# Moving the check for overfull experts into the last expert, and padding narrow tiles to 128 bytes

## The chip, the cores and the metric

The kernel runs on one NeuronCore of a Trainium2 chip. The metric is the device time of one execution in microseconds (us). TensorE (PE) does the matrix products, VectorE (DVE) and ScalarE (ACT) the elementwise work, SyncE (SP) issues nearly all transfers, and GpSimd (POOL) does a few small things.

## The reference, cut to what matters

Two decoder blocks of two layers each run on 256 tokens of width 1024. The last layer's feed-forward is a mixture of eight experts, and it is there that the change moves work:

```python
def moe_swiglu(xn, router, wg, wu, wd):
    t = xn.reshape(B * S, D)
    logits = (t @ router).astype(jnp.float32)
    top_val, top_idx = lax.top_k(logits, TOP_K)          # TOP_K = 2
    gates = jax.nn.softmax(top_val, axis=-1)
    combine = jnp.sum(jax.nn.one_hot(top_idx, N_EXPERTS) * gates[..., None], axis=1)
    out = jnp.zeros_like(t)
    for e in range(N_EXPERTS):                            # 8 experts, inner width 3584
        out = out + combine[:, e:e + 1] * swiglu(t, wg[e], wu[e], wd[e])
    return out.reshape(B, S, D)
```

All of it is float32. A gated residual with its own 1024 x 1024 matrix and a last norm follow.

## The kernel before

**Weights.** Every weight matrix is laid out beforehand in tiles of 512 x 512 (1 MB) in the order in which they are used (class Plan). `ahead` keeps up to five tiles in flight from HBM into `raw` buffers and splits each, half a tile at a time, into a high part (`hi`, a cast on ACT, L435) and a rest (`lo`, a subtraction on DVE, L436). There are five hi and five lo buffers. `mm3` then does three matmuls per block of 128 rows (L450, L451, L452): high by high, rest of the activations by high, high by rest of the weights. Activations are the stationary operand, split in the same way, weights the moving one, 512 columns wide. One tile is twelve matmuls.

**Buffers.** SBUF is cut by pools, one after the other in the order in which they open. A slot takes its bytes per partition, rounded up to 32. `n` tiles (split activations with a gain) come from a pool near the start. `l` tiles (other split activations and much else) come from the pool `lg`, which opens anew in each stage behind the pools `sec` and `sc`, and `x` tiles (the last expert's products) from `lx`. `sec`, from the second block on, holds a tile `half` of 8 bytes; `sc` of the experts' stage holds six narrow tiles that together take 288 bytes. So `l` tiles start at a multiple of 128 bytes in the first block, 32 bytes past one in the second block up to the experts, and 64 past one in the experts, as do `x` tiles.

**Experts.** At most 128 tokens are gathered for each expert (`gather`), so one pass of 128 rows does it if no expert has more. For each of seven chunks of 512 inner columns, `experts` multiplies by the gate matrix (`mg`) and the up matrix (`mu`), two tiles each, into PSUM tiles `a` from a pool of four. ACT's Silu (L1557) and a DVE product (L1559) join them, four transposes on PE (L484) with a split (L492 on ACT, L493 on DVE) turn the product over, and one chunk later `both` multiplies by two tiles of the down matrix (`md`) into two PSUM tiles y. These come from the pool of four `m` tiles, which also serves transposes and gathers. After the last chunk `scatter` splits y (L1503 on ACT, L1504 on DVE), spreads it over the tokens with eight matmuls (L1508, L1509) and adds it to x (L1511).

The seventh expert (e == MID, which is 6) ends in another way: its last chunk's down products follow at once, all outstanding tasks are drained (L1627), and `overflow` loads the largest token count into a register of every engine (L1628) and branches on it (L1661). Where some expert has over 128 tokens, a long body of some 330 instructions per expert on PE and on SP does the rest; with these inputs it is skipped. The way past it has waits of its own: each engine waits for its own earlier work to be complete, and SP for its transfers. The last expert then does its up products, all its down products after them (`finish`), and the final gate.

From the third chunk of the seventh expert on, `raw` has four buffers instead of twelve.

**What sets the order.** PE's order is as the program is written. On the other engines a scheduler moves instructions, but not past a branch. `push` queues generators, `step` and `slot` advance them between products, `need` advances them until a condition holds, `drain` until none is left.

Of the kernel before, what the change touches and what calls it, by code (L numbers as in the profile page):

```python
# [8 lines left out]
F32 = mybir.dt.float32  # L9
# [70 lines left out]
class Plan:  # L80
# [76 lines left out]
    def moe(self):  # L157
        def up(e, c):
            for key, w in (("mg", "moe_w_gate_2"), ("mu", "moe_w_up_2")):
                for g in range(2):  # L160
                    self.add((key, e, c, g), "w3", (w, 0, e), g * 512, g * 512 + 512, c * 512, 512)

        def down(e, c, h):
            self.add(("md", e, c, h), "w3", ("moe_w_down_2", 0, e), c * 512, c * 512 + 512, h * 512, 512)

        def gate(c, g):
            self.add(("pg", c, g), "w3", ("ple_gate_2", 1), g * 512, g * 512 + 512, c * 512, 512)

        prev = None
        for e in range(N_EXP):  # L170
            for c in range(N_FF):
                up(e, c)
                if prev:
                    for h in range(2):
                        down(*prev, h)
                prev = (e, c) if e < N_EXP - 1 else None
                if c == N_FF - 1 and e == MID:
                    for h in range(2):
                        down(e, c, h)
                    prev = None  # L180
        for h in range(2):
            for c in range(N_FF):
                if h and c == LATE:
                    gate(0, 0)
                down(N_EXP - 1, c, h)
        if LATE == N_FF:
            gate(0, 0)
        gate(1, 0)
        gate(0, 1)
        gate(1, 1)  # L190
# [109 lines left out]
class Kernel:  # L300
    def __init__(self, tc, io, ctx):
        self.tc = tc
        self.nc = tc.nc
        self.io = io
        pool = lambda name, bufs, **k: ctx.enter_context(tc.tile_pool(name=name, bufs=bufs, **k))
        self.const = pool("const", 1)
        self.raw_p = pool("raw", RAW)
        self.hi_p = pool("hi", NSPLIT)
        self.lo_p = pool("lo", NSPLIT)
        self.sm = pool("sm", 40)  # L310
        self.na = pool("na", 8)
        self.acc_p = pool("acc", 4, space=PSUM)
        self.ms_p = pool("ms", 4, space=PSUM)
        self.scope = None
        self.plan = Plan()
        self.specs = self.plan.specs
        self.n_dma = self.n_split = self.n_used = 0
        self.rawt = {}
        self.split = {}
        self.flip = 0  # L320
        self.urgent = []
        self.tasks = []
        self.now = 0
        self.rate = 2
        self.grain = GRAIN1
        self.fetching = 0
        self.ring = deque([self.raw_p] * RAW)
        self.queue = None
# [70 lines left out]
    def M(self, *shape):  # L399
        return self.ms_p.tile([128, *(shape or (512,))], F32, tag="m", name="m")  # L400

    def A(self):
        return self.acc_p.tile([128, 512], F32, tag="a", name="a")

    def xs(self, b, h):
        return self.xt[b][h]
# [206 lines left out]
    def fetch(self, name, dt=F32, pool=None):  # L613
        nc, src = self.nc, self.io["c_" + name]
        queue = self.queue or nc.gpsimd
        n = src.shape[1]
        t = (pool or self.sc).tile([128, n], dt, name=name)
        self.fetching += 1

        def gen():  # L620
            yield 3
            if dt == F32:
                queue.dma_start(t, src)
            else:
                for c in range(0, n, 384):
                    m = min(384, n - c)
                    r = self.T((128, m))
                    queue.dma_start(r, src[:, c:c + m])
                    nc.gpsimd.tensor_copy(t[:, c:c + m], r)
                    yield 1  # L630
            self.fetching -= 1
        self.push(gen())
        return t
# [755 lines left out]
    def route(self, norm, ms):  # L1389
        nc = self.nc  # L1390
        small = lambda name, shape, dt=F32: self.sc.tile([128, *shape], dt, name=name)
        self.comb, self.rank, self.sel = small("comb", (2, 8)), small("rank", (2, 8)), small("sel", (2, 8))
        self.count, self.most = small("count", (8,), I32), small("most", (1,), I32)
        self.rst = small("rst", (3, 2), BF16)
        self.unit = small("unit", (128,), BF16)
        nc.vector.tensor_copy(self.unit, self.ident)
        self.rows = [[[small(f"x{n}{b}{h}", (512,), BF16) for n in range(3)] for h in range(2)] for b in range(2)]
        self.need(lambda: ms[2] == 4)
        for h in range(2):
            for b in range(2):  # L1400
                self.thirds(self.xs(b, h), self.rows[b][h], self.T())
        self.spin(SPIN)
        with self.soon(HPR):
            top, s0, s1 = self.pick(ms[:2])

        def rest():
            yield 2
            cnt = self.M(8)
            for b in range(2):
                nc.tensor.matmul(cnt, self.ones, self.sel[:, b], start=b == 0, stop=b == 1)  # L1410
            self.thirds(norm.rst, [self.rst[:, n] for n in range(3)], self.S(2))
            e, g = self.S(2, 2), self.S(2, 2)
            R = norm.ready()
            for b in range(2):
                nc.vector.tensor_scalar(e[:, b, 0:1], top[:, b, 1:2], top[:, b, 0:1], R[b], op0=ALU.subtract, op1=ALU.mult)
            nc.scalar.activation(e[:, :, 1], e[:, :, 0], AF.Exp)
            nc.vector.tensor_scalar(e[:, :, 0], e[:, :, 1], 1.0, None, op0=ALU.add)
            nc.vector.reciprocal(g[:, :, 0], e[:, :, 0])
            nc.vector.tensor_mul(g[:, :, 1], g[:, :, 0], e[:, :, 1])
            for b in range(2):  # L1420
                nc.vector.tensor_scalar(s0[:, b], s0[:, b], g[:, b, 0:1], None, op0=ALU.mult)
                nc.vector.scalar_tensor_tensor(self.comb[:, b], s1[:, b], g[:, b, 1:2], s0[:, b], op0=ALU.mult, op1=ALU.add)
            most = self.S(1)
            nc.vector.tensor_reduce(most, cnt, axis=AX.X, op=ALU.max)
            nc.vector.tensor_copy(self.count, cnt)
            nc.vector.tensor_copy(self.most, most)
        self.push(rest())
# [96 lines left out]

    def both(self, y, e, c, fT, res):
        if c == 0:
            y.extend([self.M(), self.M()])
        for h in range(2):
            self.down(y[h], e, c, h, fT)
            if c == N_FF - 1:  # L1530
                self.push(self.scatter(e, y[h], h, res))

    def experts(self, inner):
# [4 lines left out]
        for e in range(N_EXP):  # L1538
# [2 lines left out]
            y, ft = [], []  # L1541
            for c in range(N_FF):
                for nm in ("mg", "mu"):
                    a = self.A()
                    for g in range(2):
                        w = self.take((nm, e, c, g))
                        self.need(lambda: act[g] is not None)
                        hi, lo = act[g]
                        for j in range(4):
                            self.mm3(a, hi[:, j], lo[:, j], *w[j], g == 0 and j == 0, g == 1 and j == 3)  # L1550
                        if g == 0:
                            self.slot()
# [17 lines left out]
                pend = (y, e, c, fT, here) if e < N_EXP - 1 else None  # L1570
                if c == 2 and e == N_EXP - 2:
                    self.ring = deque([self.raw_p] * RAW)
                if c == 4 and e < N_EXP - 1:
                    res, gen = self.gather(e + 1, 0)
                    self.push(gen)
            if e == MID:
                self.both(*pend)
                pend = None
                inner.close()
                self.overflow()  # L1580
                self.inner(self.scope, lx=2 * N_FF - 2)
        return ft, here

    def finish(self, ft, here, pp, nxt, last):
# [4 lines left out]

        def gate(c, g, b, w):  # L1590
            if (c, b) not in acc:
                acc[c, b] = self.A()
            self.need(lambda: nxt.act[b][g] is not None)
            ah, al = nxt.act[b][g]
            for j in range(4):
# [1 line left out]
            self.slot()  # L1597

        for h in range(2):
            y = self.M()  # L1600
            for c in range(N_FF):
                if h and c == LATE:
                    w = self.take(("pg", 0, 0))
# [20 lines left out]

    def overflow(self):
        nc, io = self.nc, self.io
        self.drain()  # L1627
        n = nc.values_load(self.most[0:1, 0:1], min_val=0, max_val=256)  # L1628

        def wt(key, j):  # L1630
# [4 lines left out]
        def one(e):  # L1635
# [5 lines left out]
            for c in range(N_FF):  # L1641
                accs = []
                for w in ("mg", "mu"):
                    a = self.A()
                    for k in range(8):
                        nc.tensor.matmul(a, act[k // 4][0][:, k % 4], wt((w, e, c, k // 4), k % 4),
                                         start=k == 0, stop=k == 7)
# [10 lines left out]
                for _ in self.scatter(e, y[h], h, res):  # L1658
                    pass

        with self.tc.If(n > 128):  # L1661
            for e in range(N_EXP):
                ne = nc.values_load(self.count[0:1, e:e + 1], min_val=0, max_val=256)
                with self.tc.If(ne > 128):
                    with self.tc.tile_pool(name="ov", bufs=4) as pool, self.tc.tile_pool(name="scp", bufs=4) as self.scp:
                        keep = self.lg, self.oh
                        self.lg = self.oh = pool
                        one(e)
                        self.lg, self.oh = keep


def program(tc, io, stages=("all",)):
# [73 lines left out]


MANUAL = {mybir.EngineType.PE}


def constants():
# [74 lines left out]
```

## Time and profile before

| what | value |
|---|---|
| time, median of 3 runs | 2497.12 us (2496.11 to 2497.93) |
| the profiled execution's own time | 2501.25 us |
| its span, first to last instruction | 2499.4 us |
| PE busy in it | 2464.4 us, 99% |
| DVE busy | 1922.3 us, 77% |
| ACT busy | 1618.6 us, 65% |
| weights and other bytes moved | 600.16 MB, mean 240 GB/s |

The table is the page's first part. A busy PE is not a PE at its peak: matmuls overlap, and a matmul's length is a model. Two matmuls of 512 columns start some 0.23 us apart while each is shown as 0.39 or 0.40 us long. A loss is therefore read from starts, from the idle time in square brackets, and from the granted clock.

### The profile page before, as it was taken

Reading aid. Unit: us, or ns where it says so; the run is one execution under the profiler, and the core shown is the slowest. Engines: PE = TensorE matmul, PEld = TensorE weight load, DVE = VectorE, ACT = ScalarE, POOL = GpSimd, SP = SyncE. Lnnn points to the kernel's source line nnn. Section 1 sums busy time; section 2 is a strip of 40 time slices with the busy share of each in tenths; the row PEclk is TensorE's granted clock in tenths of the full one; section 3 lists DMA queues with packets and bytes.
Section 4 is the critical chain, followed back from the end, with each engine's and each line's share of the span. In section 5 each row is a group of like instructions: output and inputs, shape, how many; then the busy total and the mean of one; then the engine's idle time right before and its main releaser. Section 6 shows DMA issues by size and latency. Waiting matters only on the chain. (4 is left out here: it accounts for less than half of the span.)

```text
span 2499.4 us, 33937 instructions
## 1 busy us (share of the span) xinstructions
PE 2464.4 (99%) x12113; PEld 2040.2 (82%) x12113; DVE 1922.3 (77%) x3330; ACT 1618.6 (65%) x2667; POOL 47.5 (2%) x66
## 2 busy tenths in 40 slices
PE   9999999999999999999999999999999999999998
PEld 7888888888888887888888878888888888888786
DVE  7775765578667656775576879999898989898888
ACT  7555555575556546654557567777777777777675
POOL 1000000100000002000001000000000000000000
PEclk9999999999999999999999989999999999999999
DMA  7443555553345555344564469999899999977895
GB/s 277 158 146 125 179 178 188 198 201 144 135 152 191 175 176 200 106 169 169 199 214 162 166 273 354 356 354 361 342 348 357 353 356 349 361 285 290 322 342 194
DMA packets 90530, 600.16 MB, mean 240 GB/s; under 512 B 12576, under 2 KB 14368, under 8 KB 19568
## 3 DMA queue, kind: packets, MB, share of 16 engines
q1 hardware_dynamic: 84240, 591.27, 64.2%
q10 hardware_dynamic: 4928, 3.16, 0.5%
q0 software_dynamic: 1184, 3.48, 0.4%
q8 instruction: 97, 1.59, 0.2%
q14 instruction: 81, 0.66, 0.1%
HBM read 596.82 MB, written 1.05 MB: 239 GB/s over the span
## 5 line engine op out<-in xcount | busy, mean ns | idle before, releaser
L436 DVE TENSOR_TENSOR lo<-raw,hi 128x512 fp32r<-128x512 f32 (+3 forms) x1584 | 1384.2, 911 | 315.9 <-ACT hi L435 296.7
L435 ACT CAST hi<-raw 128x512 fp32r<-128x512 f32 (+3 forms) x1584 | 1198.2, 800 | 422.6 <-PE a L451 340.1
L450 PE MATMUL a<-hi,n 128*128 128x512 f32 (+2 forms) x2176 | 867.9, 399 | 4.6 <-PEq L1661 3.5
L452 PE MATMUL a<-lo,n 128*128 128x512 f32 (+2 forms) x2176 | 848.9, 390 | 0.0
L451 PE MATMUL a<-hi,n 128*128 128x512 f32 (+2 forms) x2176 | 845.7, 389 | 1.7 <-DVE n L503 1.7
L452 PEld LDWEIGHTS a<-lo,n 128*128 128x128 f32 x2176 | 410.4, 189 | 93.3 <-DVE lo L436 5.1
L451 PEld LDWEIGHTS a<-hi,n 128*128 128x128 f32 x2176 | 411.7, 189 | 81.5 <-DVE n L503 3.2
L450 PEld LDWEIGHTS a<-hi,n 128*128 128x128 f32 x2176 | 411.1, 189 | 81.8 <-issue 4.2
L450 PE MATMUL a<-hi,l 128*128 128x512 f32 x552 | 220.3, 399 | 0.0
L452 PE MATMUL a<-lo,l 128*128 128x512 f32 x552 | 216.2, 392 | 0.0
L451 PE MATMUL a<-hi,l 128*128 128x512 f32 x552 | 216.1, 391 | 0.0
L492 ACT CAST l<-m 128x512 fp32r<-128x512 f32 (+1 forms) x126 | 70.2, 559 | 150.8 <-PE m L484 150.8
L450 PE MATMUL m<-hi,l 128*128 128x512 f32 x400 | 158.9, 397 | 0.7 <-ACT l L492 0.7
L451 PE MATMUL m<-hi,l 128*128 128x512 f32 x400 | 158.3, 396 | 0.2 <-DVE l L493 0.2
L452 PE MATMUL m<-lo,l 128*128 128x512 f32 x400 | 158.1, 395 | 0.0
L493 DVE TENSOR_TENSOR l<-m,l 128x512 fp32r<-128x512 f32 (+1 forms) x126 | 82.5, 658 | 62.4 <-ACT l L492 62.3
L452 PEld LDWEIGHTS a<-lo,l 128*128 128x128 f32 x552 | 103.7, 188 | 23.2
L451 PEld LDWEIGHTS a<-hi,l 128*128 128x128 f32 x552 | 103.8, 188 | 21.1
L450 PEld LDWEIGHTS a<-hi,l 128*128 128x128 f32 x552 | 103.7, 188 | 21.0
L484 PE MATMUL m<-ident,t 128*128 128x128 f32 x652 | 99.0, 272 | 2.8 <-DVE t L567 2.1
L484 PEld LDWEIGHTS m<-ident,t 128*128 128x128 f32 x652 | 80.3, 140 | 22.4 <-DVE t L567 2.6
L450 PEld LDWEIGHTS m<-hi,l 128*128 128x128 f32 x400 | 75.2, 188 | 18.4 <-ACT l L492 0.9
(302 smaller groups left out, 1784.7 us busy)
## 6 DMA issues: line engine op xcount, KB each, us to landing
raw<-in_w_dram SPq DMA_DIRECT2D x553, 1024.0 KB, 5.1
raw<-in_w_dram SPq DMA_DIRECT2D x10, 512.0 KB, 3.4
raw<-in_w_dram SPq DMA_DIRECT2D x4, 520.0 KB, 4.1
t<-in_c_dil_dram POOLq DMA_DIRECT2D x6, 192.0 KB, 2.9
x<-in_x_dram SPq DMA_DIRECT2D x4, 256.0 KB, 7.1
raw<-in_w_dram SPq DMA_DIRECT2D x4, 256.0 KB, 6.8
dec<-in_c_dec_dram POOLq DMA_DIRECT2D x2, 512.0 KB, 7.8
out_dram<-x SPq DMA_DIRECT2D x4, 256.0 KB, 2.0
```

Source lines behind the costliest of these rows:

```text
L435: nc.scalar.copy(hi[:, p], t[:, q])
L436: nc.vector.tensor_sub(lo[:, p], t[:, q], hi[:, p].bitcast(F32))
L450: mm(out, ah, wh, start=start, stop=False)
L451: mm(out, al, wh, start=False, stop=False)
L452: mm(out, ah, wl, start=False, stop=stop)
L484: self.nc.tensor.transpose(p[:, j], src[:, j * 128:(j + 1) * 128], self.ident)
L492: nc.scalar.copy(hi, p[:, :m])
L493: nc.vector.tensor_sub(lo, p[:, :m], hi.bitcast(F32))
```

## The change

The seventh expert no longer ends in a way of its own: its last down products and its scatter are carried into the last expert, as between all others. `overflow` is called in the last expert before the fourth block of 128 rows in the second `mu` tile of its third chunk, without the drain. Each engine gets an instruction that names the coming branch and calls it likely taken (the hint); it stands behind the second chunk, with a scheduling boundary that no instruction is moved past. The body of the branch has a pool for its own `tmp` tiles.

The y tiles move from the `m` pool to the PSUM pool of accumulators, which now has two names, `a` and `y`, with two buffers each; elsewhere calls take the names in turn, a, a, y, y. In the experts `mg` and `mu` share the two `a` buffers.

Narrow tiles are padded: fetched constants to 32 elements (128 bytes), the experts' narrow tiles to 384 bytes in sum; the pool of small tiles has 38 slots instead of 40. With that the `l`, `x` and `t` tiles of all stages start at a multiple of 128 bytes.

```diff
@@ class Plan, moe
-                if c == N_FF - 1 and e == MID:
-                    for h in range(2):
-                        down(e, c, h)
-                    prev = None
@@ Kernel.__init__
-        self.sm = pool("sm", 40)
+        self.sm = pool("sm", 38)
-        self.acc_p = pool("acc", 4, space=PSUM)
+        self.acc_p = pool("acc", 2, space=PSUM)
+        self.turns = 0
@@
-    def A(self):
-        return self.acc_p.tile([128, 512], F32, tag="a", name="a")
+    def A(self, tag=None):
+        if tag is None:
+            tag = "ay"[self.turns // 2 % 2]
+            self.turns += 1
+        return self.acc_p.tile([128, 512], F32, tag=tag, name="a")
@@ fetch
-        t = (pool or self.sc).tile([128, n], dt, name=name)
+        t = (pool or self.sc).tile([128, max(n, 32)], dt, name=name)[:, :n]
@@ route
-        self.count, self.most = small("count", (8,), I32), small("most", (1,), I32)
-        self.rst = small("rst", (3, 2), BF16)
+        self.count, self.most = small("count", (8,), I32), small("most", (8,), I32)[:, 0:1]
+        self.rst = small("rst", (8, 2), BF16)[:, 0:3]
+        small("rest", (24,))
@@ both
-            y.extend([self.M(), self.M()])
+            y.extend([self.A("y"), self.A("y")])
@@ experts
-                    a = self.A()
+                    a = self.A("a")
...
+                        check = e > MID and c == 2 and nm == "mu" and g == 1
                         for j in range(4):
+                            if check and j == 3:
+                                self.overflow()
                             self.mm3(a, hi[:, j], lo[:, j], *w[j], g == 0 and j == 0, g == 1 and j == 3)
...
+                if c == 1 and e > MID:
+                    self.tc.no_sync_barrier()
+                    self.tc.mark_branch_hint_location("most", "LikelyTaken", ENGINES)
...
             if e == MID:
-                self.both(*pend)
-                pend = None
                 inner.close()
-                self.overflow()
                 self.inner(self.scope, lx=2 * N_FF - 2)
@@ finish
-                acc[c, b] = self.A()
+                acc[c, b] = self.A("ay"[c])
-            y = self.M()
+            y = self.A("y")
@@ overflow
-        self.drain()
-                    a = self.A()
+                    a = self.A("y")
-        with self.tc.If(n > 128):
+        with self.tc.If(n > 128, label="most"):
...
-                        keep = self.lg, self.oh
-                        self.lg = self.oh = pool
+                        keep = self.lg, self.oh, self.tmp
+                        self.lg = self.oh = self.tmp = pool
@@
+ENGINES = tuple(getattr(mybir.EngineType, e) for e in ("PE", "Activation", "DVE", "SP", "Pool"))
```

On PE, the last instructions ahead of the branch, before the change (o is the matrix that spreads the rows over the tokens; the numbers tell buffers apart):

```order
L452 MATMUL m_21070<-lo_21912,l_21942 128x512
L1508 MATMUL m_21990<-l_21980,o_20603 128x512
L1509 MATMUL m_21990<-l_21981,o_20603 128x512
L1508 MATMUL m_21994<-l_21986,o_20603 128x512
L1509 MATMUL m_21994<-l_21987,o_20603 128x512
L1508 MATMUL m_21998<-l_21980,o_20603 128x512
L1509 MATMUL m_21998<-l_21981,o_20603 128x512
L1508 MATMUL m_22002<-l_21986,o_20603 128x512
L1509 MATMUL m_22002<-l_21987,o_20603 128x512
L1628 TENSOR_LOAD most_13866
L1661 COMPARE_AND_BRANCH
```

And after it, on PE at the hint and at the branch, which are 48 rows apart (lines are shifted by one to four):

```order
L453 MATMUL a_22151<-lo_22121,n_21696 128x512
L1510 MATMUL m_22201<-l_22110,o_20604 128x512
L1511 MATMUL m_22201<-l_22111,o_20604 128x512
L1827 BRANCH_PREFETCH_HINT
L451 MATMUL a_22211<-hi_22154,n_21638 128x512
```

```order
L453 MATMUL a_22267<-lo_22237,n_21696 128x512
L451 MATMUL a_22267<-hi_22240,n_21696 128x512
L452 MATMUL a_22267<-hi_22240,n_21697 128x512
L453 MATMUL a_22267<-lo_22241,n_21696 128x512
L1632 TENSOR_LOAD most_13866
L1665 COMPARE_AND_BRANCH
```

The eight scatter matmuls now stand in pairs among up products, and the branch stands between a block's products and the next block's, with three matmuls of the same tile behind it.

On DVE, the last expert-to-expert splits ahead of the branch, before the change (x is the running sum of the tokens):

```order
L436 TENSOR_TENSOR lo<-raw,hi 128x1024 x4
L1504 TENSOR_TENSOR l<-m,l 128x512
L436 TENSOR_TENSOR lo<-raw,hi 128x1024 x2
L1504 TENSOR_TENSOR l<-m,l 128x512
L1511 SCALAR_TENSOR_TENSOR x_81<-m,comb,x_81 128x512
L1511 SCALAR_TENSOR_TENSOR x_82<-m,comb,x_82 128x512
L1511 SCALAR_TENSOR_TENSOR x_83<-m,comb,x_83 128x512
L1511 SCALAR_TENSOR_TENSOR x_84<-m,comb,x_84 128x512
L436 TENSOR_TENSOR lo<-raw,hi 128x1024
L1628 TENSOR_LOAD most
L1661 COMPARE_AND_BRANCH
```

And after it:

```order
L1564 SCALAR_TENSOR_TENSOR t<-a,s,t 128x512
L437 TENSOR_TENSOR lo<-raw,hi 128x1024 x2
L1513 SCALAR_TENSOR_TENSOR x_84<-m,comb,x_84 128x512
L1827 BRANCH_PREFETCH_HINT
L437 TENSOR_TENSOR lo<-raw,hi 128x1024 x5
L494 TENSOR_TENSOR x<-m,x 128x512
L437 TENSOR_TENSOR lo<-raw,hi 128x1024 x2
L1632 TENSOR_LOAD most
L1665 COMPARE_AND_BRANCH
```

The four additions no longer stand in a row ahead of the branch; seven splits and one activation's rest stand between the hint and the branch.

On SP, before the change, the load of the count (which stood far ahead) and the branch:

```order
L418 DMA raw<-in_w_dram 128x1024 x2
L418 DMA raw<-in_w_dram 128x2048 x19
L1628 TENSOR_LOAD most
L1628 ISA x2
L418 DMA raw<-in_w_dram 128x2048 x284
L1661 COMPARE_AND_BRANCH
```

And after it:

```order
L419 DMA raw<-in_w_dram 128x1024 x2
L419 DMA raw<-in_w_dram 128x2048 x310
L1827 BRANCH_PREFETCH_HINT
L419 DMA raw<-in_w_dram 128x2048 x4
L1632 TENSOR_LOAD most
L1665 COMPARE_AND_BRANCH
```

SP now issues eleven more tiles ahead of the branch, loads the count there, and has four transfers between hint and branch.

## Rows read from the trace of the kernel before

**Rows 1.** The page: the span, and each engine's busy time.

```profile
span 2499.4 us, 33937 instructions
...
PE 2464.4 (99%) x12113; PEld 2040.2 (82%) x12113; DVE 1922.3 (77%) x3330; ACT 1618.6 (65%) x2667; POOL 47.5 (2%) x66
```

**Rows 2.** Stretches: length; PE, PEld, DVE, ACT, POOL busy; PE clock, DMA share, GB/s.

```profile
1840.00:1960.00 120.00, 120.00 (x574) 97.51 (x573) 108.07 (x112) 88.32 (x106) 0.00 (x0) 1.00 0.95 354
...
2353.00:2473.00 120.00, 119.70 (x541) 97.19 (x540) 108.15 (x111) 91.77 (x112) 0.00 (x0) 1.00 0.89 338
```

**Rows 3.** Timeline of PE around the branch: start, length, instruction, [idle before <-releaser].

```profile
2325.37 0.60 PE L484 MATMUL m<-ident,t 128*128 128x128 f32 x4
2326.64 0.51 PE L450 MATMUL m<-hi,l 128*128 128x512 f32 x1 [0.68 <-ACT l L492]
...
2327.71 0.40 PE L452 MATMUL m<-lo,l 128*128 128x512 f32 x1
...
2332.61 0.39 PE L452 MATMUL m<-lo,l 128*128 128x512 f32 x1
...
2335.73 0.50 PE L1509 MATMUL m<-l,o 128*128 128x512 f32 x1 [1.56 <-DVE l L1504]
...
2340.95 0.77 PE L450 MATMUL a<-hi,n 128*128 128x512 f32 x1 [3.47 <-PEq L1661]
...
2347.00 0.40 PE L452 MATMUL a<-lo,n 128*128 128x512 f32 x1
```

**Rows 4.** The branch and its waits, L1661 by engine: ns min/median/max, first and last start.

```profile
L1661 SPq EVENT_SEMAPHORE  x9: 17/17/17, 2337.3 to 2339.3; - x9
...
L1661 PEldq EVENT_SEMAPHORE  x2: 51/51/51, 2340.7 to 2340.8; - x2
...
L1661 POOLq COMPARE_BRANCH  x1: 53/53/53, 1465.4 to 1465.4; - x1
L1661 POOLq EVENT_SEMAPHORE  x1: 17/17/17, 1465.6 to 1465.6; - x1
L1661 SPq COMPARE_BRANCH  x1: 50/50/50, 2332.6 to 2332.6; - x1
...
L1661 PEldq COMPARE_BRANCH  x1: 4306/4306/4306, 2336.3 to 2336.3; - x1
```

**Rows 5.** The load of the count on PE, L1628, in the same columns.

```profile
L1628 PEldq TENSOR_LOAD <-most x1: 492/492/492, 2335.7 to 2335.7; - x1
```

**Rows 6.** Stretches for PE alone: length, PE busy, clock, DMA share, GB/s.

```profile
2340.00:2345.00 5.00, 4.04 (x10) 0.50 0.67 216
```

**Rows 7.** The same view, around an earlier gap of PE.

```profile
1053.00:1058.00 5.00, 3.68 (x25) 1.00 0.41 172
```

**Rows 8.** Groups by shape, 870 to 945 us: count | busy us, mean ns of one.

```profile
L451 PE MATMUL a<-hi,l 128*128 128x512 f32 x109 | 42.4, 389 | 0.0
```

**Rows 9.** The same view, 950 to 1470 us (second block ahead of the experts).

```profile
L451 PE MATMUL a<-hi,l 128*128 128x512 f32 x168 | 66.4, 395 | 0.0
```

**Rows 10.** The same view, 1606 to 2320 us (experts).

```profile
L450 PE MATMUL a<-hi,n 128*128 128x512 f32 x644 | 256.0, 397 | 0.0
...
L451 PE MATMUL a<-hi,n 128*128 128x512 f32 x644 | 251.4, 390 | 0.0
```

**Rows 11.** The page's costliest groups: the experts' down products.

```profile
L451 PE MATMUL m<-hi,l 128*128 128x512 f32 x400 | 158.3, 396 | 0.2 <-DVE l L493 0.2
```

**Rows 12.** Groups by shape, 2341 to 2480 us: the last expert's down products.

```profile
L451 PE MATMUL m<-hi,x 128*128 128x512 f32 x48 | 18.9, 395 | 0.0
```

**Rows 13.** Waits of PE's weight loads, 1476 to 2320 us: total, times, longest.

```profile
PEld a L452 <- DVE lo L436: 4.3, 20, 0.2
```

**Rows 14.** Waits of DVE in the same stretch.

```profile
DVE t L1559 <- PE a L452: 1.4, 1, 1.4
```

**Rows 15.** Transfers of weight tiles, L418, 2270 to 2475 us.

```profile
DMA to landing us min/median/max: 4.6/5.6/9.1
```

**Rows 16.** Waits from 2347 to 2475 us, in the columns of rows 13.

```profile
ACT hi L435 <- DMA raw<-in_w_dram: 6.2, 6, 2.3
```

More of the change, by code (lines that the diff above doesn't have):

```diff
@@ L1665, in overflow @@
                     with self.tc.tile_pool(name="ov", bufs=4) as pool, self.tc.tile_pool(name="scp", bufs=4) as self.scp:
-                        keep = self.lg, self.oh
-                        self.lg = self.oh = pool
+                        keep = self.lg, self.oh, self.tmp
+                        self.lg = self.oh = self.tmp = pool
                         one(e)
-                        self.lg, self.oh = keep
+                        self.lg, self.oh, self.tmp = keep
 def program(tc, io, stages=("all",)):
```

## The prediction, made before the changed kernel ran

> **What bounds the kernel now.** I read the page first: PE is busy in 2464 of 2499 us [rows 1], so only what makes PE's instructions start earlier or closer together can count. Next I read the stretches of the experts. In 120 us of them PE is never idle, while DVE is busy for 108 us, ACT for 88, and the transfers for 0.95 of the time [rows 2]: PE is the bound, with DVE and the transfers close behind. The timeline of PE shows the one place in the experts where PE stands still, the end of the seventh, and the rows of the branch show which engine is held there, and when [rows 3 to 6]. Last I compared the same matmul on stationary tiles that start at different places in SBUF [rows 8 to 12]. So there are two terms, the stall and the padding.
>
> **The stall and what it costs today.** From 2325.37 to 2347.00, 21.63 us, PE does four transposes, 24 down matmuls, eight scatter matmuls, and 14 up matmuls up to the first at full speed [rows 3]. Between 2327.71 and 2332.61 there are 21 starts, 0.233 us apart; the shown length of 0.40 is 0.16 longer. Without waits the stretch would be 32 x 0.233 + 14 x 0.227 + 0.44 for the transposes = 11.1 us. **10.5 us are lost.** They are: the wait for the last product's turn (0.68 shown idle), the wait for the scatter's rest (1.56), the branch (3.47), and the clock, which is at the half level (1.2 GHz) after that [rows 3, 6]: from 2340.95 to 2347.00 there are 14 starts in 6.05 us instead of 3.2, so 2.9 us are the clock's. The remainder, 1.9 us, is in drains and restarts that the modelled lengths hide.
>
> After the change the turn and the scatter stand among up products, as between all other experts, where PE does not idle [rows 2]; I take them as free. Their DVE work (two rests and four additions, 512 columns each) now falls into the last expert, whose DVE is at 108 of 120 us [rows 2], so that cover is thin.
>
> **What the branch costs at its new place.** PE's load of the count takes 0.49 us, its branch 4.31, and then two waits of 0.05 lead to the first matmul at 2340.95: 5.2 us from the load on [rows 3 to 5]. SP jumps at 2332.6 and its next instruction starts at 2337.3, 4.7 us later; POOL, which has almost no code in the body, needs 0.2 us from branch to next instruction [rows 4]. So a jump costs what it takes until the code behind it is at hand. No row shows a hint. Its effect lies between POOL's 0.2 and PE's 4.3, and I take POOL's: the hint stands 45 matmuls and four transposes, over 10 us, ahead of PE's branch, twice the longest jump. The load and the branch can pass while PE still works on what is queued, as today, where PE's last matmul ends 1.8 us after the load has begun. What cannot be hidden is the way past the body, which waits for PE's own last matmul: its end (0.16 beyond the spacing), the waits (0.1), and 0.15 from them to the next matmul, with POOL's 0.2 about 0.6 us. I take 0.7. A gap of that length does not cost the clock: at 1053 to 1058 PE idles for 1.3 us in all, at full clock [rows 7].
>
> What is queued behind the branch: on DVE and ACT the splits of the next tiles, each delayed by a load and a drain (some 0.6 us); on SP the next weight tile. SP's way past the body waits until all its transfers have landed, 5.6 us in the median after issue [rows 15], while tiles are wanted every 2.8 us (12 matmuls); so one tile comes up to 2.8 us late. Four raw buffers and five split ones stand between that and PE, but today ACT already waits six times for a landing in the last expert [rows 16]. I put this knock-on at 1.0 us, between 0 and 2.8. The stall term is then 10.5 - 0.7 - 1.0 = **8.8 us**.
>
> The Trainium skill, "Runtime: NRT & Kernel Launch", section "Instruction fetch mechanics", says that a taken branch to a page outside the two at hand waits for a fetch, and the difference between SP or PE and POOL agrees with it. The same section calls prefetch purely sequential, which would leave the hint without effect; that is the first rival below.
>
> **The padding.** `l` tiles at a multiple of 128 bytes (first block) give L451 389 ns [rows 8]; 32 bytes past one, 395 [rows 9]; 64 past, 396 for `l` and 395 for `x` [rows 11, 12]. `n` tiles, which lie at a multiple in all stages, give 390 in the middle of the experts [rows 10]. So the difference goes with the place and not with the stage, the PSUM pool or the traffic: 6 ns for each matmul with a displaced stationary tile. There are 3 x 168 = 504 of them ahead of the experts and 3 x 448 = 1344 in them [rows 9, 11, 12], 1848 x 6 ns = 11.1 us, all on a busy PE. Against the full sum: with `n` the group L450, which carries starts of groups, has 397 too [rows 10], and PE's weight loads wait 20 times for DVE's rest [rows 13], so a PE that runs faster will meet DVE more often; and in the last down products a tile's 12 x 0.227 = 2.72 us come under what transfers can do (338 GB/s at a share of 0.89 is 380 in full, 2.76 us for 1.05 MB [rows 2]). I take four fifths, **8.8 us**, from 5.5 (half) to 11.1. DVE and ACT have no slower form on these tiles that I could see, and I count nothing for them.
>
> The Trainium skill, "SBUF — State Buffer", section "Operand start alignment", makes the start a matter of what is legal, by element size alone, and says that its runs timed nothing. Read as if only that mattered, the term would be 0; the second rival has that.
>
> **At no cost.** The two PSUM names rotate a, a, y, y with two buffers each: every tile gets the buffer that was used four calls before, as in the pool of four. In the experts `mg` and `mu` reuse theirs after one chunk instead of two; the cover is the other matrix's 24 matmuls, 5.4 us (third rival). Taking y out of the `m` pool can only free it. Two small slots fewer, the boundary at the hint and POOL's early jump meet no one who waits.
>
> **Sum.** 8.8 + 8.8 = 17.6 us. The profiled execution took 2501.25 us (span 2499.4), 4.1 over the median of the three runs, 2497.12; I take the difference off both: 2483.6 for an execution like the profiled one, **2479.5 us** for the median.
>
> **Rivals.** (1) The hint does nothing. Then PE waits 3.5 us as today and runs at half clock after it (2.9): 6.3 us are not gained, 2485.8 us. For it: no row shows a hint. Against: the 10 us it has. (2) The padding gives nothing, because PE meets DVE's splits or because something else than the place makes the 6 ns: 2497.1 - 8.8 = 2488.3 us. For it: DVE's 90%; against: the pitch is the same in three stages with quite different traffic. Both together: 2494.6. (3) Slower: the two `a` buffers. If DVE's product (L1559), which frees the buffer of `mu`, comes so late that PE waits w per chunk, 56 chunks lose 56 w; the gain is gone at w = 0.31 us, and at 0.5 us the time is 2507.5. DVE does come to it late, since it waits for PE there only once in 50 chunks [rows 14]; but it would have to be over 5.4 us late, and then PE's waits for rests [rows 13] would be longer than 0.2 each.
>
> **Chances and range.** Forecast 0.63; hint without effect 0.20; padding without effect 0.10; both 0.04; slower 0.03. 0.2%, or 5.0 us, is about what a measurement of this kernel can tell from no change. Both together is 2.5 us off and counts as the same; so faster 0.93, same 0.04, slower 0.03. The low end is the stall with hardly a remainder (10.2) and the padding in full: 2475.5. The high end takes in rivals 1 and 2: 2489.
>
> **What would show it.** In the profile after: PE's branch at some 0.1 us instead of 4.3, and an idle gap under 1 us at it (right), or over 3 us with the clock at 0.50 (rival 1). L451 on `l` and `x` at 389 to 390 ns in all stages (right), or still 395 (rival 2). PE's waits for DVE's rests no longer in total than today (right), or several us more (the padding eaten up). SP's pause at the branch, and whether ACT waits longer for landings in the last expert (my 1.0). Waits of PE for L1557 or L1559 (rival 3). Wrong would be the whole sum if PE, freed of both, waited for transfers through the last expert: its four raw buffers have never been run without the pause that today lets them fill.

## The result: 16 us slower, and where it shows in the profile

The changed kernel took **2513.88 us** (median of 6 runs, 2510.79 to 2517.8) beside 2497.52 us for the kernel before on the same chip (6 runs, 2495.8 to 2501.16): ratio **1.0061**, interval 1.0050 to 1.0072. It is slower; the forecast was 2479.5 us, 17.6 us faster.

The page of the changed kernel, to be held against [rows 1]: PE is busy for 17 us longer with the same 12113 matmuls, and as busy a share of the span.

```profile
span 2511.4 us, 33936 instructions
PE 2481.3 (99%) x12113; PEld 2040.1 (81%) x12113; DVE 1921.4 (77%) x3330; ACT 1617.3 (64%) x2667; POOL 47.0 (2%) x66
```

So the loss is not a wait; the matmuls follow each other more slowly. Two stretches in which PE is never idle show it. Columns as in [rows 6], PE alone, the count of its instructions in parentheses; first the kernel before, then the changed one:

```profile
100.00:800.00 700.00, 700.00 (x3570) 1.00 0.47 166
1480.00:2300.00 820.00, 820.00 (x3921) 1.00 0.92 345
```

```profile
100.00:800.00 700.00, 700.00 (x3529) 1.00 0.46 163
1480.00:2300.00 820.00, 820.00 (x3858) 1.00 0.90 340
```

In the same 820 us of the experts PE gets through 63 instructions less, in the first 700 us through 41 less, at full clock. (The windows don't begin at quite the same instruction: 48 of the 63 are the short matmuls of one gather that now falls outside the window, so that one overstates the loss; of the 41, about 35 are 512 columns wide.) The loss is there from the first block on, where PE's matmuls are the same as before and in the same order.

The lengths of the matmul that answers to [rows 8 to 12] (now L452: count, ns min/median/max, first and last start), in the first block, the second, and the experts:

```profile
L452 PE MATMUL a<-hi,l x106: 390/393/404, 870.4 to 944.4; 128*128 128x512 f32 x106
...
L452 PE MATMUL a<-hi,l x162: 387/389/398, 1076.1 to 1452.6; 128*128 128x512 f32 x162
...
L452 PE MATMUL a<-hi,n x638: 387/393/404, 1620.6 to 2334.3; 128*128 128x512 f32 x160
L452 PE MATMUL a<-hi,l x320: 387/393/404, 1623.8 to 2326.9; 128*128 128x512 f32 x160
```

(The middle number is the median; rows 8 to 12 have means.) All these stationary tiles now start at a multiple of 128 bytes, and still only the second block's `l` has 389 ns. `n` has lost its 390 [rows 10], and `l` of the first block its 389 [rows 8]. The addresses in the built programs say what the three groups are: in the changed kernel `n`, `l` of the first block and `l` and `x` of the experts start at **128 modulo 256**, `l` of the second block at 0. Before, `n` and `l` of the first block were at 0 modulo 256, `l` of the second block at 32, `l` and `x` of the experts at 64. The two small slots of 64 bytes that the change takes away moved everything behind them by 128 bytes.

The branch went nearly as forecast. Its rows (as [rows 4]; then the hint on PE; then PE's timeline):

```profile
L1665 SPq EVENT_SEMAPHORE  x9: 17/17/17, 2389.9 to 2391.1; - x9
L1665 ACTq EVENT_SEMAPHORE  x2: 17/17/17, 2391.0 to 2391.1; - x2
L1665 DVEq EVENT_SEMAPHORE  x2: 21/21/21, 2391.4 to 2391.5; - x2
...
L1665 PEldq COMPARE_BRANCH  x1: 413/413/413, 2384.5 to 2384.5; - x1
L1665 SPq COMPARE_BRANCH  x1: 70/70/70, 2384.8 to 2384.8; - x1
L1665 ACTq COMPARE_BRANCH  x1: 68/68/68, 2386.6 to 2386.6; - x1
L1665 DVEq COMPARE_BRANCH  x1: 84/84/84, 2388.1 to 2388.1; - x1
```

```profile
L1827 PEldq BRANCH_PREFETCH_HINT  x1: 45/45/45, 2372.9 to 2372.9; - x1
```

```profile
2385.86 0.39 PE L453 MATMUL a<-lo,n 128*128 128x512 f32 x1
2386.55 0.47 PE L451 MATMUL a<-hi,n 128*128 128x512 f32 x1 [0.30 <-PEq L1665]
...
2391.74 0.40 PE L452 MATMUL a<-hi,n 128*128 128x512 f32 x1
2392.96 0.51 PE L453 MATMUL a<-lo,n 128*128 128x512 f32 x1 [0.82 <-DVE lo L437]
```

PE's jump takes 0.41 us instead of 4.31, PE idles for 0.30 us at it instead of 3.47, the clock stays at full, and one wait for DVE's rest of 0.82 us follows.

### The profile page after: what moved, and what is told of

Its sections match the earlier page's. It is cut to its first block, busy times and chain, and to the rows that moved or that the text cites. A ratio compares the mean times of both kernels' runs of the same rounds, so it can differ in the third digit from the quotient of the medians.

```text
span 2511.4 us, 33936 instructions
## 1 busy us (share of the span) xinstructions
PE 2481.3 (99%) x12113; PEld 2040.1 (81%) x12113; DVE 1921.4 (77%) x3330; ACT 1617.3 (64%) x2667; POOL 47.0 (2%) x66
## 5 line engine op out<-in xcount | busy, mean ns | idle before, releaser
L452 PE MATMUL a<-hi,n 128*128 128x512 f32 (+2 forms) x2176 | 851.8, 391 | 2.0 <-DVE n L504 2.0
L452 PEld LDWEIGHTS a<-hi,n 128*128 128x128 f32 x2176 | 410.5, 189 | 87.0 <-DVE n L504 3.2
L451 PE MATMUL a<-hi,l 128*128 128x512 f32 x952 | 379.5, 399 | 0.0
L453 PE MATMUL a<-lo,l 128*128 128x512 f32 x952 | 375.1, 394 | 0.0
L452 PE MATMUL a<-hi,l 128*128 128x512 f32 x952 | 374.9, 394 | 0.0
L453 PEld LDWEIGHTS a<-lo,l 128*128 128x128 f32 x952 | 179.1, 188 | 41.6
L452 PEld LDWEIGHTS a<-hi,l 128*128 128x128 f32 x952 | 179.4, 188 | 39.2
L451 PEld LDWEIGHTS a<-hi,l 128*128 128x128 f32 x952 | 179.3, 188 | 39.0
L502 ACT ACTIVATE n<-m,gains 128x128 fp32r<-128x128 f32 x224 | 64.8, 371 | 21.4 <-PE m L485 15.2
L504 DVE SCALAR_TENSOR_TENSOR n<-m,gains,n 128x128 fp32r<-128x128 f32 x224 | 64.9, 343 | 12.2 <-ACT n L502 11.5
L1562 ACT ACTIVATE t<-a,s 128x512 f32<-128x512 f32 x56 | 38.4, 686 | 14.0 <-PE a L453 14.0
L225 ACT ACTIVATE t<-x 128x512 bf16<-128x512 f32 x44 | 28.1, 640 | 26.4 <-DVE x L643 13.0
```

What stands on the lines that cost most here:

```text
L225: nc.scalar.activation(junk, xs, AF.Square, accum_out=self.ss[:, b, h:h + 1])
L451: mm(out, ah, wh, start=start, stop=False)
L452: mm(out, al, wh, start=False, stop=False)
L453: mm(out, ah, wl, start=False, stop=stop)
L502: nc.scalar.activation(hi[:, j], p[:, j], AF.Copy, scale=gain[:, j:j + 1])
L504: nc.vector.scalar_tensor_tensor(lo[:, j], p[:, j], gain[:, j:j + 1], hi[:, j].bitcast(F32), op0=ALU.mult, op1=ALU.subtract)
```

## The experiments

The pitch below is the mean distance from one start of a 512-column matmul of `mm3` to the next, worked out from all starts of a trace; distances over 300 ns (new groups, waits) are left out. "Place" is an address modulo 256, read from the built program. Each ratio is to the kernel before on the same chip, with its 95% interval; it does not go by the two medians alone, so that a difference by the ratio and one by the medians can lie 1 or 2 us apart.

**Two small slots less, alone.** The kernel before with

```diff
-        self.sm = pool("sm", 40)
+        self.sm = pool("sm", 38)
```

> The kernel before with 38 instead of 40 small slots and nothing else: every tile behind that pool starts 128 bytes lower, n at 128 instead of 0 modulo 256, l at 128 (first block), 160 (second) and 192 (experts) instead of 0, 32 and 64. Theory (a multiple of 256 counts, not of 128): 6336 wide matmuls on n, 228 to 232.5 ns a pitch, lose 28 us, 828 on l of the first block 3.5 us: 2529 us (2522 to 2534). Rival 1 (the two kinds of PSUM accumulators slow the matmuls): nothing here, 2497.5 within 2. Rival 2 (two small slots fewer make somebody wait): later than before too, but with idle time of PE and the old pitch of 228 ns.

Measured: 2522.23 us, ratio 1.0084 (1.0071 to 1.0098). PE is never idle in the first stretch and for 0.7 us in the second, and does as little in them as in the changed kernel:

```profile
100.00:800.00 700.00, 700.00 (x3532) 1.00 0.47 163
1480.00:2300.00 820.00, 819.28 (x3876) 1.00 0.90 341
```

Pitch on `n` 232.7 ns in the first block instead of 229.0. One number in one line costs 21 us by the ratio, more than the changed kernel loses, without the PSUM tiles and without a wait. I had expected a loss of 31.5 us (2529 us). It is some 10 us less, because `n` lost 3.7 to 4.3 ns a matmul and not 4.5, and because `l` of the experts, now at 192, got faster (229.6 ns instead of 233.3).

**The PSUM accumulators alone**, in the kernel before, with the names `a` and `y` given out as in the change:

```diff
-        self.acc_p = pool("acc", 4, space=PSUM)
+        self.acc_p = pool("acc", 2, space=PSUM)
...
-            y.extend([self.M(), self.M()])
+            y.extend([self.A("y"), self.A("y")])
```

> The kernel before with the changed kernel's accumulators alone (two buffers of a and two of y, the down products in y), all SBUF addresses as before. Theory of 256 bytes: 2497.5 us within 2, pitch on n 228 ns. Rival 1 (PSUM): all of the loss that is left once the branch's gain of some 9 us is taken off, 2520 to 2523 us, pitch 232.5 ns. Rival of the prediction (two buffers in the experts are too few): idle time of PE ahead of the first product of an a in the experts, 56 times, up to 20 us.

Measured: 2499.84 us, ratio 1.0004 (0.9995 to 1.0013): nothing. The two buffers of `a` cost nothing in the experts either.

```profile
100.00:800.00 700.00, 700.00 (x3570) 1.00 0.48 166
1480.00:2300.00 820.00, 820.00 (x3920) 1.00 0.91 345
```

**Two slots less again**, in the changed kernel, so that the places come back to 0:

```diff
-        self.sm = pool("sm", 38)
+        self.sm = pool("sm", 36)
```

> The changed kernel with 36 instead of 38 small slots: everything behind them another 128 bytes lower, so that n, l of the first block, l and x of the experts start at multiples of 256, l of the second block at 128. Theory of 256 bytes: 28 us back on n, 3.5 on l of the first block, 6 on the experts' l and x, 2 lost on l of the second block: 2478 us (2474 to 2484). Rival 1 (PSUM): 2514 us within 3. Rival 2 (too few small slots): 2514 or later.

Measured: **2481.21 us**, ratio 0.9927 (0.9914 to 0.9941). Against the changed kernel's 1.0061 that is 0.0134 x 2498 = 33 us for 128 bytes. The stretches, and the lengths in the experts:

```profile
100.00:800.00 700.00, 700.00 (x3570) 1.00 0.47 166
1480.00:2300.00 820.00, 820.00 (x3961) 1.00 0.92 348
```

```profile
L452 PE MATMUL a<-hi,n x635: 387/389/398, 1600.2 to 2299.5; 128*128 128x512 f32 x159
...
L452 PE MATMUL a<-hi,l x320: 389/389/398, 1602.0 to 2292.9; 128*128 128x512 f32 x160
```

**All stationary tiles at 0**, the second block's `l` too: as the last, with a filler of 128 bytes in `sec`, from which two of the experts' narrow tiles are then cut.

```diff
-        self.comb, self.rank, self.sel = small("comb", (2, 8)), small("rank", (2, 8)), small("sel", (2, 8))
+        self.comb, self.rank, self.sel = self.two[:, 0:2], self.two[:, 2:4], small("sel", (2, 8))
...
     k.second()
+    k.two = k.sec.tile([128, 4, 8], F32, name="two")
```

> As the run with 36 slots, and a filler of 128 bytes ahead of the second block's tiles, its place taken from the experts' small tiles: every wide moving operand at a multiple of 256 bytes. Theory of 256 bytes: another 2 to 3 us on 828 matmuls on l of the second block, 2475.5 us (2471 to 2482). Rival 1 (PSUM): 2514 us within 3.

Measured: 2480.59 us, ratio 0.9918 (0.9905 to 0.9932). The pitch of the second block's `l` went from 232.5 to 227.8 ns, which over its 468 counted starts is 2.2 us; the medians, 0.6 us apart, cannot show that. The same kernel once more, on the chip of the next three runs (its label names a run that it was to stand beside):

> The run with every tile at a multiple of 256 once more, beside the one without hints on the same chip: ratio to before 0.992 (0.990 to 0.994) by every theory. The hints are in it.

Measured: **2480.04 us**, ratio 0.9927 (0.9913 to 0.9940). This version beats both kernels.

**The places alone**, in the kernel before: the paddings, 36 slots and the filler, with the branch and the PSUM tiles as before.

```diff
-        self.sm = pool("sm", 40)
+        self.sm = pool("sm", 36)
...
-        t = (pool or self.sc).tile([128, n], dt, name=name)
+        t = (pool or self.sc).tile([128, max(n, 32)], dt, name=name)[:, :n]
...
     k.second()
+    k.two = k.sec.tile([128, 4, 8], F32, name="two")
```

> The kernel before with the changed kernel's paddings, 36 small slots and the filler, so that every wide stationary tile starts at a multiple of 256 bytes; branch and PSUM tiles as before. Theory of 256 bytes: 1344 matmuls on l and x of the experts 233.4 to 226.9 ns a pitch (8.7 us), 828 on l of the second block 230.7 to 227.2 (2.9 us), 11.6 us in all, the stall of 10.5 us at the branch as before: 2487 us (2485 to 2490) beside 2498. Rival (a faster PE meets DVE and transfers, four fifths or less): 2489 to 2492. Rival (all of the gain of the aligned run was the branch): 2498.

Measured: 2489.46 us, ratio 0.9958 (0.9944 to 0.9972), 10.5 us (7 to 14) by the ratio. From PE's last gap ahead of the experts (its start) to its last matmul's end, this kernel takes 1015.0 us, the one with the branch moved (the repeated run above, with the same places) 1006.3: the move is worth **8.7 us**. The medians say 9.4. That is one execution of each; three others with the branch moved and all tiles of this stretch at the same distances take 1006.5 (both at 128, below), 1007.6 (36 slots) and 1008.7 us (the first run of this version), so a gain of 6.3 to 8.7 us is what the traces show.

**Weights at 128**, stationary tiles as with 36 slots: is it the stationary operand's place that counts?

```diff
+        self.odd = pool("odd", 1)
+        self.odd.tile([128, 32], F32, name="odd")
         self.raw_p = pool("raw", RAW)
...
-        self.sm = pool("sm", 38)
+        self.sm = pool("sm", 34)
```

> The changed kernel with a filler of 128 bytes ahead of raw, hi and lo and 34 small slots: weights (the moving operand and what it is split from) start at 128 modulo 256, stationary tiles as in the run with 36 slots (0, in the second block's l 128). Theory (only the stationary operand's place counts): 2481 us within 3, pitch 227 to 228.5 ns. Rival (any operand's place): 9336 wide matmuls lose some 4.4 ns each, 41 us, 2522 us, pitch 232.

Measured: 2517.23 us, ratio 1.0073 (1.0059 to 1.0087). My theory, as it stood there, fell, and the rival was near: the stationary tiles lie at 0 and the matmuls are slow.

```profile
100.00:800.00 700.00, 700.00 (x3526) 1.00 0.46 163
1480.00:2300.00 820.00, 819.27 (x3864) 1.00 0.90 340
```

```profile
L454 PE MATMUL a<-hi,n x639: 387/393/404, 1620.1 to 2335.0; 128*128 128x512 f32 x160
```

But the second block's `l`, at 128 like the weights, had 227.8 ns. That suggested that the distance between the two operands counts, and not the place of either.

**Both at 128.** The filler of 128 bytes with 36 slots: every place of the run with 36 slots plus 128.

```diff
+        self.odd = pool("odd", 1)
+        self.odd.tile([128, 32], F32, name="odd")
         self.raw_p = pool("raw", RAW)
...
-        self.sm = pool("sm", 38)
+        self.sm = pool("sm", 36)
```

> The changed kernel with 36 small slots and a filler of 128 bytes ahead of raw, hi and lo: every place is the one of the run with 36 slots plus 128. Weights at 128 modulo 256, n, l of the first block, l and x of the experts at 128 too, l of the second block at 0. Theory D (what counts is the distance modulo 256 between the stationary and the moving tile, here 0, in the second block's l 128): 2481 us within 3, pitch 227 to 229 ns. Theory A (each operand has to start at a multiple of 256): the loss of the changed kernel at least, 2514 us, and 2550 if the two add up, pitch 232 or more.

Measured: 2480.41 us, ratio 0.9924 (0.9910 to 0.9937): as with both at 0. No operand of these matmuls but the second block's `l` (232.5 ns) starts at a multiple of 256 here, and that one is the slow one.

```profile
100.00:800.00 700.00, 700.00 (x3575) 1.00 0.47 165
1480.00:2300.00 820.00, 820.00 (x3963) 1.00 0.92 348
```

```profile
L454 PE MATMUL a<-hi,n x636: 387/389/398, 1600.1 to 2299.6; 128*128 128x512 f32 x159
...
L454 PE MATMUL a<-hi,l x320: 389/389/398, 1603.2 to 2293.6; 128*128 128x512 f32 x160
```

**Other distances.** The changed kernel with 39 slots; with 35 slots and a filler of 64 bytes ahead of the weights; and the version with all tiles at 0, with its stationary tiles moved to 224. The pools of the three, in this order:

```diff
-        self.sm = pool("sm", 38)
+        self.sm = pool("sm", 39)
```

```diff
+        self.odd = pool("odd", 1)
+        self.odd.tile([128, 16], F32, name="odd")
         self.raw_p = pool("raw", RAW)
...
-        self.sm = pool("sm", 38)
+        self.sm = pool("sm", 35)
```

```diff
-        self.sm = pool("sm", 36)
+        self.sm = pool("sm", 39)
+        self.odd = pool("odd", 1)
+        self.odd.tile([128, 8], F32, name="odd")
```

> The changed kernel with 39 small slots: n, l of the first block and l and x of the experts at 192 modulo 256, l of the second block at 64. Theory A (the last 64 bytes ahead of a multiple of 256 cost little, as 229.1 ns on l of the experts in the run with 38 slots): 1 ns on 7164 matmuls and 2 ns on 1344 more than in the run with 36 slots, 2491 us (2487 to 2495). Theory B (every place off 256 costs the same 4.4 ns): 2514 us within 4.

> The changed kernel with a filler of 64 bytes ahead of raw, hi and lo and 35 small slots: weights at 64 modulo 256, stationary tiles as in the run with 36 slots. Theory D with a sign (stationary less moving, 192 here, 64 in the second block's l): as the run with the stationary tiles at 192, 2492 us within 4, n at 229.4 ns. Without a sign (64 apart is 64 apart, as the experts' l before, 233.3 ns): 2520 us. Theory A: 2514 to 2522 us.

> The run with every tile at a multiple of 256, with all stationary tiles 32 bytes ahead of a multiple instead (39 small slots and 32 bytes more), weights at multiples of 256. Theory D says that only the distance counts, 224, of which there is no row yet: if the cost falls from 192 on to 0 (229.4 to 228.5 ns) 2480 to 2490 us, if 32 off costs what 32 past costs (233.2 ns on l of the second block) 2520 us.

Measured: 2491.94 us (ratio 0.9971, 0.9960 to 0.9982), 2488.78 us (0.9964, 0.9950 to 0.9977) and 2522.61 us (1.0093, 1.0078 to 1.0109). Stationary tiles at 192 and weights at 64 with the stationary ones at 0 come out alike, as a distance of 192 should; 224 is among the slow ones. All runs together, by the distance of the stationary from the moving tile (stationary less moving, modulo 256):

| distance | pitch in ns | where |
|---|---|---|
| 0 | 226.8 to 229.2 | `n` before 228.2 to 229.0, in the PSUM run 228.1 to 229.2; experts' `l` with 36 slots 226.8; both at 128: `n` 228.2 to 228.7 |
| 32 | 233.2 | second block's `l` before |
| 64 | 233.2 to 233.4 | experts' `l` and `x` before; second block's `l` with weights at 64 or tiles at 64 |
| 128 | 232.4 to 233.2 | `n` in the changed kernel 232.6 to 232.7; `n` with weights at 128 232.6 to 233.0 |
| 160 | 233.5 | second block's `l` with 38 slots before |
| 192 | 228.9 to 229.6 | `n` at 192 229.2 to 229.4; `n` with weights at 64 229.3 to 229.5 |
| 224 | 233.1 to 233.3 | the last run |

96 was not run. That the modulus is 256 and not 512 shows in `n`: its distance modulo 512 is 0 in the kernel before and 256 with 36 slots, and its pitch is the same (228.2 to 229.0 and 228.3 to 229.0 ns). One more rival, that PE meets what ACT and DVE read and write while they split the next weights, the starts can settle: in the distances on `n` during which no instruction of ACT, DVE or POOL runs, the mean is 227.2 ns before (263 of them) and 232.5 in the changed kernel (278). With no transfer under way either, few are left, but with the same difference: 228.5 (18) and 233.1 (21). Why 192 is nearly as good as 0 and 64 is not, the runs don't say; nor do they say whether a matmul's weights meet its own stationary tile or the next one's, whose load PE does beside it.

**No hints**, with all tiles at 0. The boundary at the hints goes with them, so the two are not separated:

```diff
-                if c == 1 and e > MID:
-                    self.tc.no_sync_barrier()
-                    self.tc.mark_branch_hint_location("most", "LikelyTaken", ENGINES)
...
-        with self.tc.If(n > 128, label="most"):
+        with self.tc.If(n > 128):
```

> The run with every tile at a multiple of 256, without the five hints and the boundary at them. If the hints are what shortened the branch: PE's branch 4.3 us instead of 0.4, 3 to 4 us of idle PE and up to 3 us of half clock more, 2483 to 2487 us. If the new place does it (work queued ahead, or nothing): 2480 us within 2.

Measured: 2484.79 us, ratio 0.9937 (0.9924 to 0.9951), beside 2480.41 for the run with both at 128. The two intervals overlap; the profile decides. The branch, PE's timeline, and three stretches (length, PE busy, clock):

```profile
L1662 PEldq COMPARE_BRANCH  x1: 4446/4446/4446, 2356.5 to 2356.5; - x1
```

```profile
2356.24 0.40 PE L453 MATMUL a<-lo,n 128*128 128x512 f32 x1
2361.24 0.76 PE L451 MATMUL a<-hi,n 128*128 128x512 f32 x1 [4.60 <-PEq L1662]
2361.80 0.63 PE L452 MATMUL a<-hi,n 128*128 128x512 f32 x1
```

```profile
2352.00:2357.00 5.00, 4.64 (x20) 1.00 0.46 188
2357.00:2362.00 5.00, 0.76 (x2) 0.74 0.88 336
2362.00:2367.00 5.00, 5.00 (x15) 0.57 0.87 313
```

PE's jump is back at 4.4 us, PE idles for 4.6, and then starts matmuls 0.43 us apart at the half level of the clock (1.2 GHz). From the last gap ahead of the experts to PE's end it is 1011.8 us instead of 1006.3 to 1008.7 in the four executions with hints: the hints are worth 3.1 to 5.5 us, and the move without them 3.2.

## Why the prediction was wrong

**The step that failed** is the padding's "multiple of 128 bytes", and with it the sentence that two small slots fewer meet no one who waits. The rows were read rightly: the difference of 6 ns goes with the place, not with stage, pool or traffic; the PSUM run and the places alone bear that out. But the tiles that I called aligned were all at a distance of 0 modulo 256 from the weights, and the other rows at 32 and 64 [rows 8 to 12]. 128 itself was in no row. I took the modulus from the words of the change, and then asked of the smaller pool only who might wait for a slot, not where it puts everything that opens behind it. With the addresses worked out modulo 256 the open question would have been visible: the change puts nearly every tile at 128, and the trace had timed 0, 32 and 64.

What that did, from the starts counted in the traces and the pitches before and after: `n` lost 2172 x 3.7 ns, 1045 x 4.55 and 2600 x 3.9 in the three stages, 23.0 us; `l` of the first block 1094 x 4.7, 5.1 us; `l` of the second block won 468 x 5.3, 2.5 us, and the experts' `l` and `x` 0.9. That is 24.7 us lost in place of 8.8 gained. With the branch's 6.3 to 8.7 us it gives 16.0 to 18.4 slower, against 16.4 between the medians and 15.2 by the ratio.

**The size of the padding term, done rightly,** was 10.5 us by the ratio (7 to 14), and 10.8 by starts and pitches (468 x 5.4, 1189 x 6.5, 133 x 4.5). By the count the four fifths were too careful; the interval of the ratio takes in 8.8 and 11.1 alike. (Two slips of the sum are too small to matter: four fifths of 11.1 is 8.9, and the low end is 2475.8 by its own terms.) PE's weight loads waited for DVE's rests 22 times, 4.2 us in all, over the experts of the repeated run, as before [rows 13].

```profile
PEld a L453 <- DVE lo L437: 4.2, 22, 0.2
```

**The stall term held,** 6.3 to 8.7 us in single executions and 9.4 by the medians, against 8.8. Its parts: 0.30 us shown idle at the branch (0.46 by starts: 2385.86 to 2386.55 less a pitch), where I had 0.7 with all drains; the turn and the scatter cost PE no idle time; the knock-on, which I put at 1.0 between 0 and 2.8, was one wait for DVE of 0.82 us here and 1.15 in the repeated run, but in the first run of that version, the same program, PE's waits for DVE's rests behind the branch come to 2.5 us instead of 1.5. So it changes from execution to execution, and that it came out near 1.0 is in part luck. My reason for it was off: I had ACT and DVE held by a load and a drain, 0.6 us, but from branch to last wait ACT is held for 4.5 us, DVE for 3.4 and SP for 6.3, much as before (5.4, 3.1 and 6.7). For SP's row before see [rows 4]; those of ACT and DVE are:

```profile
L1661 ACTq EVENT_SEMAPHORE  x2: 17/17/17, 2339.8 to 2339.9; - x2
L1661 DVEq EVENT_SEMAPHORE  x2: 21/21/21, 2341.3 to 2341.4; - x2
...
L1661 ACTq COMPARE_BRANCH  x1: 50/50/50, 2334.5 to 2334.5; - x1
...
L1661 DVEq COMPARE_BRANCH  x1: 72/72/72, 2338.3 to 2338.3; - x1
```

ACT did wait for landings more often in the last expert, 14 times instead of 6 [rows 16], and PE met that one wait, besides one of 0.3 us further on that the kernel before has too:

```profile
ACT hi L436 <- DMA raw<-in_w_dram: 11.4, 14, 2.3
```

**The rivals.** The hint without effect is refuted by the run without hints (0.41 against 4.45 us on PE). Its price of 6.3 us leaves in the 0.7 that the forecast already had at the branch; without it, it is 5.7, and the profiles show 3.1 to 5.5. The Trainium skill, "Runtime: NRT & Kernel Launch", section "Instruction fetch mechanics", where prefetch is purely sequential, does not cover this hinted branch. The two `a` buffers cost nothing by the PSUM run. "The padding gives nothing" was nearest to the truth, but was bounded at zero: I had excluded a loss from a step that moves every tile.

The forecast of 2479.5 us is nearly what the version with all tiles at 0 takes (2480.6 and 2480.0). That is in part luck, since there the padding gave 10.8 us by the count and the stall 6.3 to 8.7. The stall's mechanism was right. Of the padding's only this was right, that a displaced stationary tile slows its matmuls and by how much; what it is displaced against, I had wrong, and so the changed kernel got the opposite of the gain.

## What to carry to other kernels

Before a pool's size or a tile's width is changed, list the start addresses of all tiles that a busy TensorE reads, before and after, and compare the stationary with the moving ones modulo a larger power of two than the one under discussion. A place that no row has timed is an unknown with a cost on both sides; here 1.3% of the time (33 us) hung on 128 bytes in a pool of scratch slots. Where the same matmuls become slower everywhere and nobody waits, count instructions per stretch and look at addresses before looking at the schedule.

## What was not expected of the hardware

- The distance modulo 256 between the stationary and the moving operand sets the pitch of 128x512 float32 matmuls on a busy PE: 227 to 229 ns at 0, 229 to 230 at 192, 232 to 234 at 32, 64, 128, 160 and 224. Weight loads are shown 187 or 188 ns long (median) in all of them. The Trainium skill, "SBUF — State Buffer", section "Operand start alignment", makes the start a question of what is legal; no run here contradicts that, and 33 us hang on starts that are all legal.
- The hint shortened PE's jump from 4.45 to 0.41 us. On ACT, DVE and SP, which carried it too, the time from the branch to the last wait behind it was not shorter with it (5.3, 4.0 and 6.7 us in the repeated run with all tiles at 0) than without (2.6, 3.2 and 6.7 us, the same places). What holds them was not separated.
